# Dense operands at multiples of 512 bytes, per-head sums from two fp32r parts, and new work estimates for the weave

## The chip, the cores and the metric

One core of one Trainium2 chip runs the whole program in one launch. The metric is the device time of one execution in microseconds (us); of several executions the median counts. Smaller is better.

## The reference, cut to what matters

Two transformer blocks in a row, 512 tokens, width 1024, everything in fp32. The first has compressed, selected and windowed attention, a second attention over indexed keys, and a squared-ReLU feed-forward of 4096. The second has a half-weighted SwiGLU feed-forward of 2816, a mixer, and another such SwiGLU. The mixer is what matters for the change, because in it totals over the 64 features of each head are taken again and again:

```python
q = rms_norm_2(sb_q.reshape(B, S, SB_HEADS, HEAD_DIM), sb_q_norm[l])
k = rms_norm_2(sb_k.reshape(B, S, SB_HEADS, HEAD_DIM), sb_k_norm[l])
o_sb = stick_breaking_attention(q, k, v)
o_sb = rms_norm_2(o_sb, sb_out_norm[l].reshape(SB_HEADS, HEAD_DIM)).reshape(B, S, SB_WIDTH)
...
kk = kk / jnp.maximum(jnp.linalg.norm(kk, axis=-1, keepdims=True), 1e-12)
y = rwkv7_recurrence(r, heads(decay), kf, v, -kk, kk * a)
mean = jnp.mean(y, axis=-1, keepdims=True)
var = jnp.mean(jnp.square(y - mean), axis=-1, keepdims=True)
bonus = jnp.sum(r * kf * r_k.astype(jnp.float32), axis=-1, keepdims=True) * v
```

All the rest of the work that matters here is products of 512 tokens with weight matrices.

## The kernel before, in words

**Dense products.** Activations lie transposed, 128 features by 512 tokens to a tile. Each fp32 operand is split in two fp32r parts (high, and low as the remainder), and a product is made of three: high by high, high by low, low by high. `dense` (L352) and `dense_steps` (L362) issue them; a weight block of 128x128 is the stationary operand and an activation tile of 128x512 the moving one. All go through `mm` (L336), so in the profile all have line L339 and are told apart by their tiles: `hh`/`hl` are parts of block inputs, `oh`/`ol` of attention outputs, `uh`/`ul` and `vh`/`vl` of the two kinds of hidden feed-forward tiles, `whi`/`wlo` of weights. `Stream` (L201) loads 1 MB of weights at a time on SP's queue into one of two buffers, ScalarE copies 128x1024 of it to `whi` (L243), VectorE subtracts for `wlo` (L249), one chunk ahead.

The dense work, in blocks of 192 products (8 output tiles, 8 input tiles, 3 products each): 1.875 for the first block's projections from `h` (15 tiles of 24), 1 for its output projection (half of it from tiles of another pool, see below), 8 for the first feed-forward (4 from `hh`/`hl`, 4 from `uh`/`ul`), for each SwiGLU 5.5 up and gate (from `hh`/`hl`) and 2.75 down (from `vh`/`vl`), 3.25 for the mixer's projection and 1 for its output, both from `hh`/`hl`.

**Where tiles lie.** Memory of a partition is given out in stacks, one from the low end and one from the high end ("right"). Every tile is rounded up to 32 bytes. Adding up the tiles gives where each begins, as bytes past a multiple of 512:

- Low end: 16,512 bytes of constants and scratch, then the pool `cst` of 2,368 bytes, so the weight buffers `p32`, the parts `whi`/`wlo` (`phl`), and the temporaries `tmp` begin at 448. Above them in block 1's feed-forward come `x` and `y` at 448, then `g1` (L1280) of 32 bytes, so `uh`/`ul` begin at 480. In the SwiGLU there is no such tile, and `vh`/`vl` begin at 448.
- High end: `hp` with the 16 tiles `hh`/`hl` begins at 480 (it also holds the second half of `oh`/`ol`). Under it lies `cst1` with `gs` (L675), and under that, in block 1 only, `gp` with the first half of `oh`/`ol`, which begin at 0.

**The mixer.** `mix2` (L1681) weaves several chains of small steps with dense products as fillers. The order is made at build time by `weave` (L425): it keeps a modelled clock, to which `mm` adds each product's estimated time and `after` (L468) each step of another engine, runs the chain whose next step is due, and fills with dense products in between, so that these are used up evenly over an estimated amount of chain work, `WORK` (L23), one number for each of five stages. Chains are `rw_solve` (L1809), `rw_scan` (L1962), `sb_steps`' `norm` (L1460), `stick_head` (L1523) and `stick_out` (L1586). Each takes totals over the heads' features as a product with `blk`, a 128x128 matrix of two blocks of ones (tile `c` in the profile, being a slice of the constant table `c2`, L1687): 20 times in `root` (L491), which then forms a reciprocal root with ScalarE and VectorE, 4 times in `rw_solve` for the bonus (L1869), 4 times in `rw_scan` for the mean (L2015). `blk` and what it multiplies are plain fp32, and each such product is two passes. Only one `root` is in progress at a time (`self.roots`), and its temporaries come from 5 buffers used in turn (`tmp`, L605).

The two lines that split and multiply, and the one that takes a total:

```python
self.mm(ps, wh, xh, start=first and k == 0)
self.mm(ps, wh, xl)
self.mm(ps, wl, xh, stop=last and k == n - 1)
...
self.mm(ss, self.blk, x, start=True, stop=True)
```

Of the kernel before, what the change touches and what calls it, by code (L numbers as in the profile page):

```python
# [9 lines left out]
F32 = mybir.dt.float32  # L10
F32R = mybir.dt.float32r
BF = mybir.dt.bfloat16
I32 = mybir.dt.int32
AF = mybir.ActivationFunctionType
OP = mybir.AluOpType
# [3 lines left out]
T = 512  # L19
LA = 1  # L20
TICK, BUSY = 1707, 2100
BURST, MINR = 4, 0.002
WORK = (31e3, 43e3, 45e3, 43e3, 90e3)  # L23
SEM, SEM2, MINF = 250, 50, 4
COST = {"V": (60, 1.07), "S": (60, 0.86), "P": (60, 2.3)}
LHV = (0, 1, 2)
# [267 lines left out]
class K:  # L294
# [196 lines left out]
    def root(self, bank, x, scale, eps, floor=None):  # L491


        V, S = self.nc.vector, self.nc.scalar
        yield lambda: self.roots < 1
        self.roots += 1
        ss = self.bank(bank)
        self.mm(ss, self.blk, x, start=True, stop=True)
        v, l, r = (self.tmp(n) for n in ("rs_v", "rs_l", "rs_r"))
        if floor is None:  # L500
            S.activation(v, ss, AF.Identity, scale=scale, bias=eps)
            w = self.after("S", 512)
        else:
            V.tensor_scalar(v, ss, floor, None, op0=OP.max)
            w = self.after("V", 512)
        S.activation(l, v, AF.Ln)
        S.activation(r, l, AF.Exp, scale=-0.5)
        S.activation(l, r, AF.Square)
        self.after("S", 512, w)
        yield self.after("S", 1024) + 120  # L510
        V.scalar_tensor_tensor(v, v, -0.5, l, op0=OP.mult, op1=OP.mult)
        yield self.after("V", 512)
        V.scalar_tensor_tensor(r, v, 1.5, r, op0=OP.add, op1=OP.mult)
        yield self.after("V", 512)
        return r

    def rsqrt(self, v, l, r, out=None):
        nc = self.nc
# [83 lines left out]
            for ps, w in zip((pa, pb), ws):  # L602
                self.dense(ps, tuple(p[:, 128 * k:128 * k + 128] for p in w), [x], k == 0, k == n - 1)

    def tmp(self, name, tag="t"):  # L605
        return self.tp.tile([128, T], F32, name=name, tag=tag, bufs={"t": 5, "rt": 2}[tag])

    def dump(self, name, src):
        if name in self.dbg:
# [3 lines left out]
    def setup(self, es):  # L613
        tc, nc, a = self.tc, self.nc, self.a
# [8 lines left out]
        c2 = [1024, 1024]  # L623
# [22 lines left out]
        for n, ks in enumerate(OUT2):  # L646
            m = 8 if len(ks) < 3 else 4
# [4 lines left out]
        cp = self.ces.enter_context(tc.tile_pool(name="cst1", bufs=1, side="right"))  # L652
# [13 lines left out]
        C = {k: cst[:, o:e] for k, (o, e) in COFF.items()}  # L666
# [5 lines left out]
        nc.vector.tensor_copy(cz[:, :, 0:1], self.vec("c", 0, 8).unsqueeze(2))  # L672
        self.cz = cz
        self.modc = cp.tile([128, 48], F32, name="modc")
        self.gs = cp.tile([128, 8], F32, name="gs")  # L675
        wap = self.xin.enter_context(tc.tile_pool(name="wap", bufs=1))
        self.wq = self.xin.enter_context(tc.tile_pool(name="wq", bufs=4))
        self.ada0 = deque()
        for n, u in enumerate((0, 1, 4, 5, 2, 3, 6, 7)):
            t = wap.tile([128, 2048], F32, name=f"wa{u}", tag="wa", bufs=WAB)  # L680
# [5 lines left out]
        V, S = nc.vector, nc.scalar  # L686
        ss = self.bank("o")
# [13 lines left out]
        for nm, src, n in (("identb", C["ident"], 128), ("causalb", C["causal"], 128), ("cmaskb", C["cmask"], 256)):  # L701
            t = (c0 if nm == "identb" else cp).tile([128, n], BF, name=nm)
# [30 lines left out]

    def open_h(self):
        self.hes = ExitStack()
        self.hp = self.hes.enter_context(self.tc.tile_pool(name="hp", bufs=8, side="right"))

    def ada_part(self, cg, bank="s"):
# [170 lines left out]
    def block1_attn(self):  # L909
        tc, nc, a, ws = self.tc, self.nc, self.a, self.ws  # L910
        V, S, P = nc.vector, nc.scalar, nc.gpsimd
        x = self.xT
# [5 lines left out]
        ss, sq = self.ss0  # L918
# [81 lines left out]
        for kq in range(4):  # L1000
            hi, lo = ws.get()
            for k2 in range(2):
                k = 2 * kq + k2
# [125 lines left out]
        for i in (1, 2, 3):  # L1129
            w = work[:, WOFF[i] + 128 * i:WOFF[i] + 128 * i + 128]  # L1130
            P.affine_select(out=w, in_=w, pattern=[[-1, 128]], compare_op=OP.is_ge, fill=FILL, base=0,
                            channel_multiplier=1)
        m8 = self.ap.tile([128, 3, 8], F32, name="m8")
        dmask = self.ap.tile([128, 1152], BF, name="dmask")
        top = deque()

# [132 lines left out]
    def block1_ffn(self, oT):  # L1269
        tc, nc, a, ws = self.tc, self.nc, self.a, self.ws  # L1270
        V, S, P = nc.vector, nc.scalar, nc.gpsimd
# [5 lines left out]
        es = ExitStack()  # L1277
        fp = es.enter_context(tc.tile_pool(name="fp", bufs=1))
        y = [fp.tile([128, T], F32, name=f"y{k}") for k in range(8)]
        g1 = fp.tile([128, 8], F32, name="g1")  # L1280
        V.tensor_tensor(g1, self.modc[:, 16:24], self.vec("g_post_mix", 0, 8), op=OP.mult)
        self.gain("g_pre_ffn", 32)

# [16 lines left out]
        t = self.small("ssx")  # L1300
# [14 lines left out]
        for k in range(8):  # L1315
            t, t2 = (fp.tile([128, T], F32, name=n, tag=n, bufs=XB) for n in ("xr", "xg"))
# [364 lines left out]
    def mix2(self):  # L1681
# [2 lines left out]
        es = ExitStack()  # L1684
        cp = es.enter_context(tc.tile_pool(name="cst2", bufs=1))
        self.o2p = self.rpool = cp
        c2 = cp.tile([128, CARR2.shape[1]], F32, name="c2")  # L1687
        nc.scalar.dma_start(c2, a["cst2"])
        C = {k: c2[:, o:e] for k, (o, e) in COFF2.items()}
        self.C2 = C  # L1690
        mb = cp.tile([128, MARR.shape[1]], BF, name="mb")
        for o in range(0, MARR.shape[1], T):
# [2 lines left out]
            nc.scalar.dma_start(m[:, :e - o], a["mask2"][:, o:e])  # L1695
            V.tensor_copy(mb[:, o:e], m[:, :e - o])
        C.update({k: mb[:, o:e] for k, (o, e) in MOFF.items()})
        self.blk = C["blk"]
        self.sbmask = cp.tile([128, 128], BF, name="sbmask")
        V.tensor_copy(self.sbmask, C["sbmask"])  # L1700
        self.sbtri = cp.tile([128, 128], F32R, name="sbtri")
# [107 lines left out]
    def rw_solve(self, f, u, ag):  # L1809
# [4 lines left out]
        t2 = self.rt  # L1814
# [14 lines left out]
        for half in (0, 1):  # L1829
# [9 lines left out]
            S.activation(w(ee), pv[:, :, 1], AF.Exp)  # L1839
            for _ in range(3):  # L1840
                self.after("S", 256)
        dec = t2("dec", 8)
        V.tensor_copy(dec, ch(ei)[:, :, 63])
        yield x

# [17 lines left out]
        r = u[f, 0]  # L1863
        V.scalar_tensor_tensor(bo, r, self.vec("rw_r_k_2", f), kf, op0=OP.mult, op1=OP.mult)
        yield self.after("V", 512)
        yield lambda: (f, 2) in u
        v = u[f, 2]
        ss = self.bank("c")
        self.mm(ss, self.blk, bo, start=True, stop=True)  # L1869
        vt = tok(2, v)  # L1870
        ar = self.rp.tile([128, 8, 2, 64], F32, name="ar", tag="ar", bufs=2)
        V.tensor_tensor(ar[:, :, 1], ch(r), ch(ei), op=OP.mult)
# [89 lines left out]
    def rw_scan(self, f, u, o, g2, sg, w):  # L1962
# [48 lines left out]
                st = ns  # L2011

        yield x
        m = self.bank("pt")
        self.mm(m, self.blk, y, start=True, stop=True)  # L2015
        V.scalar_tensor_tensor(y, m, -1.0 / 64, y, op0=OP.mult, op1=OP.add)
        yield lambda: not self.squares
        self.squares = 1
# [57 lines left out]
```

## Time and profile before

| what | value |
|---|---|
| median of 3 runs | 1977.7 us (1977.63 to 1981.84) |
| the profiled execution's own time | 1968.61 us |
| its span | 1966.8 us |
| PE busy | 1890.1 us, 96% of the span |
| DVE, ACT, POOL busy | 1077.4, 781.3, 149.5 us |
| granted TensorE clock, mean | 0.983 |

The span runs from the first to the last instruction of the program; the time has 1.8 us more around it. PE is TensorE's matmuls, PEld its weight loads, DVE VectorE, ACT ScalarE, POOL GpSimd. The end of a matmul is modelled, so the length of one says little; how far apart the starts of a run of them lie is what counts. In the chain of waits, a stretch of equal products stands as one line with start, length and count, and length over count is the spacing. A line of code belongs to all its instructions, so products are told apart by tiles.

### The profile page before, as it was taken

The numbers are of one execution on the slowest core, as the hardware profiler recorded it, in microseconds if no ns is written. First come the engines' busy times: TensorE is split into PE (matmuls) and PEld (weight loads), VectorE is DVE, ScalarE is ACT, GpSimd is POOL, SyncE is SP. The second block draws the span as 40 slices with busy tenths as digits, with TensorE's granted clock in tenths as the row PEclk, the third lists the DMA queues.
The fourth block names the chain that finished last, engine by engine and source line by source line (L and its number), as shares of the span: only waits on it lengthen the run. The fifth ranks groups of instructions, "written<-read, shape, count | busy, mean of one in ns | idle before, by whom it ended". The sixth has DMA issues, their size and how long they took to land.

```text
span 1966.8 us, 27713 instructions
## 1 busy us (share of the span) xinstructions
PE 1890.1 (96%) x11556; PEld 1446.8 (74%) x11556; DVE 1077.4 (55%) x1814; ACT 781.3 (40%) x1357; POOL 149.5 (8%) x117
## 2 busy tenths in 40 slices
PE   5989999989999998999999999999999999999999
PEld 2766666768888886788888877776666778888887
DVE  7588875573334345543443456666677674344343
ACT  3666777343323133322222354242345652222221
POOL 3341110040000001000000000000002300000000
PEclk8999999989999998999999999999999999999999
DMA  7124124312223222222223231011010023232322
GB/s 298 57 94 134 74 67 148 122 50 91 102 86 107 86 88 83 72 100 87 106 86 107 72 129 61 30 42 45 23 34 33 22 86 107 86 107 86 101 86 91
DMA packets 27342, 171.56 MB, mean 87 GB/s; under 512 B 3152, under 2 KB 3408, under 8 KB 9040
## 3 DMA queue, kind: packets, MB, share of 16 engines
q1 hardware_dynamic: 23472, 163.44, 23.7%
q10 hardware_dynamic: 3744, 6.34, 1.0%
q8 instruction: 91, 1.49, 0.3%
q14 instruction: 35, 0.29, 0.0%
HBM read 167.67 MB, written 2.10 MB: 86 GB/s over the span
## 4 chain that ended last, share of the span: by engine, by line
PE 79%; DVE 3%; ACT 2%; issue 1%; POOL 1%; DMA 0%; POOLq 0%; ACTq 0%; DVEq 0%
PE ps_mm L339 44%; PE ps_s L339 23%; PE ps_c L339 6%; PE ps_pt L339 4%; PE ps_o L339 1%; PE ps_pt L890 1%; POOL xr L1320 0%; DVE wlo L249 0%; ACT whi L243 0%; POOL x L1369 0%; DMA x<-in_x 0%; PE ps_mm L746 0%; DVE hl L1384 0%; DVE y L1368 0%; POOL hl L1327 0%
## 5 line engine op out<-in xcount | busy, mean ns | idle before, releaser
L243 ACT ACTIVATE whi<-w 128x1024 fp32r<-128x1024 f32 (+4 forms) x277 | 274.7, 994 | 771.3 <-PE ps_mm L339 466.1
L339 PE MATMUL ps_mm<-hh,whi 128*128 128x512 f32 x1304 | 526.8, 405 | 21.4 <-ACT whi L243 9.1
L339 PE MATMUL ps_mm<-hh,wlo 128*128 128x512 f32 x1304 | 526.6, 404 | 6.1 <-DVE wlo L249 6.1
L339 PE MATMUL ps_mm<-hl,whi 128*128 128x512 f32 x1304 | 526.6, 404 | 3.2 <-DVE hl L1327 1.5
L249 DVE TENSOR_TENSOR wlo<-w,whi 128x1024 fp32r<-128x1024 f32 (+7 forms) x316 | 321.8, 1026 | 158.3 <-ACT whi L243 157.9
L339 PEld LDWEIGHTS ps_mm<-hh,whi 128*128 128x128 f32 x1304 | 247.0, 190 | 89.2 <-ACT whi L243 12.4
L339 PEld LDWEIGHTS ps_mm<-hh,wlo 128*128 128x128 f32 x1304 | 247.2, 190 | 73.4 <-DVE wlo L249 9.9
L339 PEld LDWEIGHTS ps_mm<-hl,whi 128*128 128x128 f32 x1304 | 247.0, 189 | 69.2 <-issue 4.7
L339 PE MATMUL ps_s<-vl,whi 128*128 128x512 f32 x352 | 137.2, 390 | 0.0
L339 PE MATMUL ps_s<-vh,wlo 128*128 128x512 f32 x352 | 137.0, 389 | 0.0
L339 PE MATMUL ps_s<-vh,whi 128*128 128x512 f32 x352 | 136.8, 389 | 0.0
L1425 DVE TENSOR_TENSOR su<-ps_mm,rr 128x512 f32<-128x512 f32 x42 | 29.0, 690 | 139.8 <-PE ps_mm L339 139.8
L1437 DVE SCALAR_TENSOR_TENSOR x<-ps_s,x 128x512 f32<-128x512 f32 x48 | 33.2, 691 | 129.2 <-PE ps_s L339 129.2
L339 PE MATMUL ps_s<-uh,wlo 128*128 128x512 f32 x256 | 101.1, 395 | 0.0
L339 PE MATMUL ps_s<-uh,whi 128*128 128x512 f32 x256 | 101.1, 395 | 0.0
L339 PE MATMUL ps_s<-ul,whi 128*128 128x512 f32 x256 | 101.1, 395 | 0.0
L1424 DVE TENSOR_TENSOR sg<-ps_mm,rr 128x512 f32<-128x512 f32 x42 | 29.0, 691 | 103.9 <-PE ps_mm L339 99.7
L339 PEld LDWEIGHTS ps_s<-vl,whi 128*128 128x128 f32 x352 | 66.1, 188 | 14.3 <-DVE vl L771 0.6
L339 PEld LDWEIGHTS ps_s<-vh,wlo 128*128 128x128 f32 x352 | 66.1, 188 | 13.9
L339 PEld LDWEIGHTS ps_s<-vh,whi 128*128 128x128 f32 x352 | 66.1, 188 | 13.8
L1361 DVE TENSOR_TENSOR y<-y,ps_s 128x512 f32<-128x512 f32 x24 | 16.5, 687 | 74.0 <-PE ps_s L339 74.0
L339 PEld LDWEIGHTS ps_s<-uh,wlo 128*128 128x128 f32 x256 | 48.0, 187 | 11.8
(569 smaller groups left out, 2710.2 us busy)
## 6 DMA issues: line engine op xcount, KB each, us to landing
w<-in_gu SPq DMA_DIRECT2D x44, 1024.0 KB, 4.9
w<-in_win SPq DMA_DIRECT2D x17, 1024.0 KB, 5.0
w<-in_wada SPq DMA_DIRECT2D x16, 1024.0 KB, 5.4
w<-in_wup SPq DMA_DIRECT2D x16, 1024.0 KB, 4.9
w<-in_wdn SPq DMA_DIRECT2D x16, 1024.0 KB, 4.9
w<-in_dn SPq DMA_DIRECT2D x16, 1024.0 KB, 4.9
wa<-in_wada SPq DMA_DIRECT2D x8, 1024.0 KB, 13.6
w<-in_dn SPq DMA_DIRECT2D x8, 768.0 KB, 4.3
```

The costliest lines, as they stand in the source:

```text
L243: self.nc.scalar.activation(hi[:, :n], src, AF.Copy)
L249: self.nc.vector.tensor_tensor(lo[:, o:m], src[:, o:m], hi[:, o:m], op=OP.subtract)
L339: self.last_pe = self.nc.tensor.matmul(o, l, r, start=start, stop=stop, skip_group_check=True)
L890: nc.tensor.transpose(b[:, x:x + 128], p[:, po:po + 128], self.ident)
L1361: V.tensor_tensor(y[m], y[m], ps, op=OP.add)
L1424: V.tensor_tensor(g, pg, r, op=OP.mult)
L1425: V.tensor_tensor(v, pu, r, op=OP.mult)
L1437: V.scalar_tensor_tensor(self.x[m], ps, 0.5, self.x[m], op0=OP.mult, op1=OP.add)
```

## The change

- **Layout.** `gs` grows from 32 to 64 bytes, `m8` from 96 to 128, `g1` from 32 to 512; a pool of 480 bytes is put above `hp`; `dec` (twice 32 bytes) moves from the mixer's pool into `cst`. The constant table `c2` is cut in two: its first 1,536 bytes go into a temporary and only the rest stays, while `blk` gets 512 bytes of its own. By the same sums `whi`/`wlo`, `hh`/`hl`, `oh`/`ol`, `uh`/`ul` and `vh`/`vl` now all begin at 0 past a multiple of 512.
- **Totals.** `head_sums` splits the tile in a high and a low fp32r part (a ScalarE copy, a VectorE subtraction, two temporaries) and multiplies `blk`, now fp32r, with each. It takes the place of the fp32 product in all 28 places. In `rw_solve` it comes before the wait for the value tile instead of after it.
- **Estimates.** The five numbers of `WORK` go down by 3,000 to 5,000.

```diff
-WORK = (31e3, 43e3, 45e3, 43e3, 90e3)
+WORK = (28e3, 40e3, 41e3, 40e3, 85e3)
...
-        ss = self.bank(bank)
-        self.mm(ss, self.blk, x, start=True, stop=True)
+        ss = yield from self.head_sums(bank, x)
...
+    def head_sums(self, bank, x):
+        hi, lo = (self.tmp(n, dt=F32R) for n in ("hs_h", "hs_l"))
+        self.nc.scalar.activation(hi, x, AF.Copy)
+        yield self.after("S", 512)
+        self.nc.vector.tensor_tensor(lo, x, hi, op=OP.subtract)
+        yield self.after("V", 512)
+        ss = self.bank(bank)
+        self.mm(ss, self.blk, hi, start=True)
+        self.mm(ss, self.blk, lo, stop=True)
+        return ss
...
-        self.gs = cp.tile([128, 8], F32, name="gs")
+        self.gs = cp.tile([128, 16], F32, name="gs")[:, :8]
...
+        self.hes.enter_context(self.tc.tile_pool(name="pad", bufs=1, side="right")).tile([128, 120], F32, name="pad")
...
-        m8 = self.ap.tile([128, 3, 8], F32, name="m8")
+        m8 = self.ap.tile([128, 4, 8], F32, name="m8")[:, :3]
...
-        g1 = fp.tile([128, 8], F32, name="g1")
+        g1 = fp.tile([128, 128], F32, name="g1")[:, :8]
...
-        c2 = cp.tile([128, CARR2.shape[1]], F32, name="c2")
-        nc.scalar.dma_start(c2, a["cst2"])
-        C = {k: c2[:, o:e] for k, (o, e) in COFF2.items()}
+        n1 = COFF2["cum"][0]
+        c1 = self.tmp("c1")
+        nc.scalar.dma_start(c1[:, :n1], a["cst2"][:, :n1])
+        c2 = cp.tile([128, CARR2.shape[1] - n1], F32, name="c2")
+        nc.scalar.dma_start(c2, a["cst2"][:, n1:])
+        C = {k: c1[:, o:e] if o < n1 else c2[:, o - n1:e - n1] for k, (o, e) in COFF2.items()}
...
-        self.blk = C["blk"]
+        self.blk = cp.tile([128, 128], F32R, name="blk")
+        V.tensor_copy(self.blk, C["blk"])
...
-        dec = t2("dec", 8)
+        dec = self.small("dec", 8)
...
+        ss = yield from self.head_sums("c", bo)
         yield lambda: (f, 2) in u
         v = u[f, 2]
-        ss = self.bank("c")
-        self.mm(ss, self.blk, bo, start=True, stop=True)
...
-        m = self.bank("pt")
-        self.mm(m, self.blk, y, start=True, stop=True)
+        m = yield from self.head_sums("pt", y)
```

## Rows read from the trace of the kernel before

**Rows 1.** The page: span, busy time of each engine.

```profile
span 1966.8 us, 27713 instructions
PE 1890.1 (96%) x11556; PEld 1446.8 (74%) x11556; DVE 1077.4 (55%) x1814; ACT 781.3 (40%) x1357; POOL 149.5 (8%) x117
```

**Rows 2.** Stretches: start:end, length, busy of PE, PEld, DVE, ACT, POOL, clock, DMA.

```profile
0.00:341.00 341.00, 300.34 (x1694) 208.88 (x1694) 245.91 (x560) 218.40 (x488) 80.70 (x67) 0.96 0.35 126
...
419.00:767.00 348.00, 347.96 (x1484) 279.44 (x1484) 138.54 (x153) 105.73 (x136) 6.72 (x4) 0.99 0.27 94
...
808.00:1152.00 344.00, 344.00 (x1490) 278.98 (x1489) 154.34 (x184) 99.96 (x120) 0.00 (x0) 1.00 0.27 95
...
1191.00:1450.00 259.00, 257.10 (x3899) 184.57 (x3898) 172.99 (x358) 93.85 (x191) 0.00 (x0) 1.00 0.11 37
1450.00:1570.00 120.00, 115.08 (x755) 81.84 (x754) 83.78 (x169) 71.78 (x148) 29.23 (x24) 0.99 0.09 30
...
1607.00:1963.00 356.00, 355.94 (x1544) 288.47 (x1542) 150.22 (x177) 94.50 (x111) 0.00 (x0) 1.00 0.27 94
```

**Rows 3.** The chain that ended last: start, length, engine, tile, line, count.

```profile
453.72 44.80 PE ps_s L339 x192
498.52 44.80 PE ps_mm L339 x192
...
875.55 43.55 PE ps_s L339 x192
919.10 89.60 PE ps_mm L339 x384
```

**Rows 4.** Timeline of PE, first block's output projection: start, length, instruction.

```profile
349.64 0.39 PE L339 MATMUL ps_mm<-oh,whi 128*128 128x512 f32 x1
...
352.39 0.40 PE L339 MATMUL ps_mm<-oh,whi 128*128 128x512 f32 x1
...
355.18 0.39 PE L339 MATMUL ps_mm<-oh,whi 128*128 128x512 f32 x1
```

**Rows 5.** The same view in the mixer: one total, and what follows it.

```profile
1200.40 1.02 PE L339 MATMUL ps_c<-bo,c 128*128 128x512 f32 x2
1201.35 1.15 PE L339 MATMUL ps_c<-ident,u 64*64 64x64 f32 x32
```

**Rows 6.** Groups by line and tile: totals' passes, a root's step, a split.

```profile
L339 PE MATMUL ps_c<-bo,c x8: 592/592/697, 1200.4 to 1397.8; 128*128 128x512 f32 x8
...
L506 ACT ACTIVATE rs_l<-rs_v 128x512 f32<-128x512 f32 x20 | 12.6, 628 | 2.6 <-DVE rs_v L504 2.2
...
L1617 ACT ACTIVATE hh<-orw x4: 620/622/631, 1467.1 to 1495.7; 128x512 fp32r<-128x512 f32 x4
...
L1619 DVE TENSOR_TENSOR hl<-orw,hh x4: 677/684/1220, 1468.9 to 1496.3; 128x512 fp32r<-128x512 f32 x4
L1619 DVE TENSOR_TENSOR hl<-sq,hh x4: 681/954/1523, 1525.0 to 1577.7; 128x512 fp32r<-128x512 f32 x4
```

**Rows 7.** The chain that ended last, in the mixer's last stage.

```profile
1541.72 0.83 DVE rs_v L511
...
1543.15 0.60 DVE rs_r L513
```

**Rows 8.** Weight loads, the constants' load and copy, and ACT's longest wait.

```profile
w<-in_gu SPq DMA_DIRECT2D x44, 1024.0 KB, 4.9
...
c<-in_cst ACTq DMA_DIRECT2D x1, 320.0 KB, 2.8
...
L1702 DVE CAST sbtri<-c x1: 219/219/219, 1155.4 to 1155.4; 128x128 fp32r<-128x128 f32 x1
...
ACT whi L243 <- PE ps_mm L339: 466.1, 147, 9.5
```

More of the change, by code (lines that the diff above doesn't have):

```diff
@@ L603, in dense2, with tmp @@
                 self.dense(ps, tuple(p[:, 128 * k:128 * k + 128] for p in w), [x], k == 0, k == n - 1)
-    def tmp(self, name, tag="t"):
-        return self.tp.tile([128, T], F32, name=name, tag=tag, bufs={"t": 5, "rt": 2}[tag])
+    def tmp(self, name, tag="t", dt=F32):
+        return self.tp.tile([128, T], dt, name=name, tag=tag, bufs={"t": 5, "rt": 2}[tag])
     def dump(self, name, src):
```

## The prediction

> **What bounds the kernel now.** I read the page first. TensorE (PE) is busy for 96% of the span, VectorE for 55%, ScalarE for 40% [rows 1]: a change counts as far as it shortens what PE does, or makes PE wait. Then the stretches [rows 2]. In the first feed-forward and both SwiGLUs PE has no idle time (344.00 of 344.00 us in the third row), while VectorE is busy for under half; in the mixer from 1191 to 1450 PE is busy for 257.10 of 259.00. Two stretches differ: the first 341 us (PE 300.34) and the mixer's end, 1450 to 1570 (PE 115.08 of 120, with VectorE at 83.78). The granted clock is 1.00 in the full ones, the upper level, 2.4 GHz. The supply isn't late: a megabyte of weights lands in 4.9 us and feeds 48 products, some 11 us of PE, and ScalarE waits 466.1 us in all for PE before it may split more weights [rows 8].
>
> So the spacing of dense products matters, and the chain of waits gives it in blocks of 192 [rows 3]. The reader is to see two prices for the same work. The blocks from `uh`/`ul` and from `hh`/`hl` take 44.80 us, 233.3 ns a product. The block from `vh`/`vl` at 875.55 takes 43.55 us, 226.8 ns. Line, shapes and types are the same, both `ps_s` blocks have the same loop around them, and the weights begin at 448 in all; what differs is that `uh`, `ul`, `hh`, `hl` begin at 480 past a multiple of 512 bytes and `vh`, `vl` at 448. The output projection shows a third place [rows 4]: its first 12 products come from tiles at 0, and (352.39 - 349.64) / 12 = 229.2 ns; the next 12, from tiles at 480, take (355.18 - 352.39) / 12 = 232.5 ns. The floor is a column a cycle, 512 / 2.4 = 213.3 ns, 40.96 us a block; no row comes near it.
>
> **Layout: the first and largest term.** After the change both operands begin at 0. No row shows that pair. Moving at 480 with weights at 448 is 233.3, 448 with 448 is 226.8, 0 with 448 is 229.2. Bounds: 213.3 ns below (no loss at all), 233.3 above (the place doesn't matter). I take 226.8. The pair (0, 0) is nearest to (448, 448) in the one thing that orders the three rows: there moving and stationary operand begin at the same place in a 512-byte stretch, and that row is the fastest; moving one alone to 0 made it worse, so 0 by itself has no merit that a row shows. Then:
> - `hh`/`hl`/`uh`/`ul` blocks in full stretches: 8 in the first feed-forward, 2 x 5.5 in the SwiGLUs, 3.25 and 1 in the mixer, 23.25; each saves 44.80 - 43.55 = 1.25 us.
> - First block's projections, 1.875 blocks, and half of its output projection: PE isn't always the bound there, so half of 2.375 counts, 1.2.
> - `vh`/`vl`, 5.5 blocks: already at 226.8, nothing.
>
> 24.45 x 1.25 = **30.6 us saved**. With faster products the splits must keep up; VectorE and ScalarE have half of each full stretch free, so nothing is late next.
>
> **Totals from two parts.** Removed: 28 fp32 products of two passes. The two records of one span 1.02 us and one lasts 592 ns [rows 5, 6], so the passes are 0.43 apart, 0.86 in all; from its start to the next product's it is 0.95, hand-over included. I take 0.86. Added: two fp32r products, 2 x 0.227 = 0.45. PE saves 0.41 each. Added beside PE: a ScalarE copy, 0.62 as at L1617, and a VectorE subtraction, 0.68 as at L1619 in the median, both in front of the sum, so each chain step grows by 1.30 less 0.41. In a full PE stretch the fillers cover that: 20 of the 28 lie in 1191 to 1450, where the additions raise VectorE from 173 to 187 us of 259. There 20 x 0.41 = 8.1 us are saved. The other 8 lie in 1450 to 1570, where the chain runs through VectorE steps of roots in places [rows 7]; PE's 3.3 us are saved at most, 8 x 1.30 = 10.4 are added at most. I take half of the 10.4 as exposed, 2 us net lost. Sum: **6.1 saved**; bounds 11.4 saved (all hidden) and 2.3 lost (the end fully exposed). The five `root` temporaries now fill the ring of 5 buffers once; a write could wait for the reader five tenants back. Such a wait would sit on ScalarE or VectorE ahead of the weight splits, and it lies inside the bound above as long as PE has split weights in hand.
>
> **Estimates.** The modelled clock changes the order alone. PE's idle time in the two weave stretches is 1.9 and 4.9 us; better pacing can remove at most these 6.8, worse pacing may add about as much again. I take nothing.
>
> **Constants.** One load becomes two on ScalarE's queue, and `blk` is copied once more by VectorE: 0.22 us as `sbtri` [rows 8], beside PE. If the new load landed late, VectorE's queue would hold the splits behind the copies for up to another 2.8 us. I take nothing: in the trace that load lands 2.8 us after its issue [rows 8], with PE running meanwhile. `dec`, `m8`, `gs`, `g1` and the pad change addresses only.
>
> **Sum.** 30.6 + 6.1 = 36.7 us. Against the profiled execution's own time: 1968.6 - 36.7 = 1931.9. The median of the runs stands 9.1 above that execution; the same saving from the median gives **1941 us**. A measurement here tells about 0.2% (4 us) from no change.
>
> **Rivals.**
> - *No loss at 0 (faster than forecast).* If what costs 13 to 20 ns over 213.3 is that an operand begins away from 0, both being there takes it away. For it: every weight tile in the trace is off 0, so no row contradicts it. Against: moving one operand to 0 cost 2.4 ns more than 448. At the floor 24.45 x 3.84 + 5.5 x 2.59 = 108, with totals 114: 1864 us; half way to the floor 69 and 6: 1902. Chance 0.32. The Trainium skill, TensorE: Matmul & The Clock Gate, Back-to-back issue gap, gives N / 2.4 + 2.5 ns for a warm product, 215.7 for 512 columns; the trace disagrees (226.8 at best), and by that page's figure the time would be an estimated 1877.
> - *The place gives little.* If 0 acts as in [rows 4], 229.2 ns, the 24.45 blocks save 0.80 each and the 5.5 lose 0.45: 17 and 6, 1955 us. If it gives nothing, only the totals are left: 1972. For it: the one row with an operand at 0. Against: that row has weights at 448. Chance 0.12. The Trainium skill, SBUF — State Buffer, Specifications (TRN2), has lines of 16 bytes; by that, 480, 448 and 0 are equally good, and the time would be 1972. The trace disagrees: 44.80 against 43.55.
> - *The longer totals become the bound of the weave (slower).* Copy and subtraction stand in front of all 28 sums, one root at a time. For it: a like subtraction took up to 1523 ns in the mixer's end [rows 6]. Exposed at that length a total costs 0.62 + 1.52 - 0.41 = 1.73 us, all 28 of them 48.4: 1977.7 - 30.6 + 48.4 = 1996. It decides from 18 exposed totals on. Against: 20 of 28 lie where PE always has fillers. Chance 0.06.
>
> **How the numbers follow.** Forecast 0.50 (its own range 1928 to 1955: the totals' and pacing bounds, with the runs' own spread), no loss 0.32, little 0.12, slower 0.06. The range for 8 in 10 reaches from near the floor, 1866, to 1956, the better half of "little". Faster by over 0.2%: the first two and most of the third, 0.91. Within 0.2%: 0.03. Slower: 0.06.
>
> **What would show it.** Right: blocks of 192 at 43.5 us in the chain for all tile names, the first feed-forward's stretch near 338 us instead of 348, 56 fp32r products with `blk` in place of 56 fp32 passes, PE still without idle time from 1191 to 1450. Blocks at 41 to 42 mean the first rival, 44.0 or more the second. PE idle time in the mixer that grows past some 15 us, behind ScalarE copies or VectorE subtractions of the totals, means the third. The forecast is wrong if blocks at (0, 0) are not near 43.55.

## The result, and the profile after

The changed kernel takes **1955.6 us** in the median of 4 runs (1951.5 to 1957.0) against 1979.8 for the kernel before (4 runs): ratio 0.987, 95% interval [0.985, 0.990], 24 us less. A second set on another occasion gave 1960.0 against 1976.7, ratio 0.991 [0.990, 0.993]. The forecast was 36.7 us less, 1941; both results are faster than before by more than a measurement tells, and by less than forecast. The first lies outside the forecast's own range (1928 to 1955) and 0.4 us inside the range for 8 in 10 (up to 1956), the second outside both.

The page of the changed kernel, its span and busy times, against [rows 1]:

```profile
span 1949.7 us, 27795 instructions
PE 1864.8 (96%) x11552; PEld 1456.1 (75%) x11556; DVE 1094.1 (56%) x1843; ACT 797.5 (41%) x1385; POOL 149.9 (8%) x117
```

TensorE lost 25 us of busy time, but the span only 17.1: 8 us of new idle time. Which stage it is shows in the chain that ended last (start, length, engine, tile, line, count), against [rows 3]:

```profile
450.44 43.52 PE ps_s L339 x192
493.96 43.52 PE ps_mm L339 x192
...
861.98 43.52 PE ps_s L339 x192
905.50 87.04 PE ps_mm L339 x384
```

Every block of 192 dense products now takes 43.52 us, 226.7 ns a product, whatever tile it reads; the forecast took 226.8. So the loss is not in the dense stages. The time itself, 1955.6, is that of the rival "the place gives little" (1955), but these blocks rule that rival out: it needs 44.0 us or more. The stretches show it (start:end, length, busy time and instructions of PE, PEld, DVE, ACT, POOL, granted clock, DMA share, GB/s), against [rows 2]:

```profile
417.01:755.00 337.99, 337.99 (x1484) 279.58 (x1484) 138.59 (x153) 105.81 (x137) 6.70 (x4) 1.00 0.29 97
796.70:1133.97 337.27, 337.27 (x1489) 279.03 (x1488) 154.31 (x183) 99.74 (x120) 0.00 (x0) 1.00 0.28 97
1133.97:1608.44 474.47, 457.14 (x5010) 336.64 (x5010) 325.88 (x651) 229.47 (x453) 29.57 (x24) 0.98 0.14 46
1171.00:1431.00 260.00, 251.03 (x3738) 185.62 (x3736) 179.70 (x368) 106.91 (x213) 0.00 (x0) 0.99 0.11 37
1431.00:1551.00 120.00, 114.32 (x884) 84.48 (x885) 87.97 (x173) 70.85 (x147) 29.57 (x24) 0.94 0.06 21
```

The first feed-forward's stretch is 338.0 us where 348 stood, the SwiGLU 337.3 where 344 stood, both with TensorE busy throughout. The third row is the whole mixer, from the end of the first SwiGLU's last block to the first block of the second. It takes 474.5 us, against 466.7 (1152.3 to 1619.0) in the profiled execution of before; the forecast's terms (5.3 from the layout, 6.1 from the totals) make it 455.3. Inside it, the weave's stretch now has 260.00 - 251.03 = 9.0 us of idle TensorE (1.9 before), and in the mixer's end the granted clock is 0.94 (0.99 before).

So the span's 17.1 us are 2.0 before the first feed-forward, 9.6 up to the SwiGLU, 6.7 and 6.5 in the two SwiGLUs, 24.8 in all, less 7.8 lost in the mixer. The runs below ask where those 7.8, and the 11.4 that were forecast there, went.

To compare mixers, each is split in three: TensorE's idle time; what the clock cost (the mixer cut into stretches of 5 us, each one's length times one minus its granted clock, summed); and the rest, the work at the upper level, 2.4 GHz (with whatever short waits the modelled ends of matmuls hide). In us, one profiled execution a row:

| kernel | mixer | idle | clock | rest |
|---|---|---|---|---|
| before | 466.7 | 8.4 | 1.7 | 456.6 |
| before, profiled again | 473.9 | 8.2 | 10.3 | 455.5 |
| layout alone | 470.7 | 8.8 | 6.8 | 455.0 |
| layout and estimates | 469.8 | 10.8 | 3.4 | 455.6 |
| totals alone | 473.2 | 14.6 | 8.5 | 450.1 |
| changed, old estimates | 474.2 | 16.7 | 8.6 | 448.9 |
| **changed** | 474.5 | 17.4 | 10.3 | 446.9 |
| changed, profiled again | 479.9 | 17.2 | 17.2 | 445.6 |
| low parts on GpSimd | 483.1 | 21.7 | 13.7 | 447.7 |
| `bo` totals undone | 464.7 | 12.9 | 3.4 | 448.5 |
| `bo` and `y` totals undone | 465.3 | 12.7 | 3.4 | 449.2 |

### The profile page after: what moved, and what is told of

It reads as the page before. It is cut to its first block, busy times and chain, and to the rows that moved or that the text cites. A ratio compares the mean times of both kernels' runs of the same rounds, so it can differ in the third digit from the quotient of the medians.

```text
span 1949.7 us, 27795 instructions
## 1 busy us (share of the span) xinstructions
PE 1864.8 (96%) x11552; PEld 1456.1 (75%) x11556; DVE 1094.1 (56%) x1843; ACT 797.5 (41%) x1385; POOL 149.9 (8%) x117
## 4 chain that ended last, share of the span: by engine, by line
PE 77%; DVE 3%; ACT 2%; POOL 1%; issue 1%; DMA 1%; ACTq 0%; POOLq 0%
PE ps_mm L339 43%; PE ps_s L339 23%; PE ps_c L339 5%; PE ps_pt L339 4%; PE ps_o L339 1%; ACT whi L243 1%; DVE wlo L249 1%; POOL xr L1332 0%; PE ps_pt L902 0%; POOL x L1381 0%; DMA mask<-in_mask 0%; DMA x<-in_x 0%; PE ps_mm L758 0%; DVE hl L1396 0%; DVE rs_v L510 0%
## 5 line engine op out<-in xcount | busy, mean ns | idle before, releaser
L339 PE MATMUL ps_mm<-hh,whi 128*128 128x512 f32 x1304 | 519.9, 400 | 20.9 <-ACT whi L243 9.5
L339 PE MATMUL ps_mm<-hh,wlo 128*128 128x512 f32 x1304 | 518.1, 398 | 6.2 <-DVE wlo L249 6.2
L339 PE MATMUL ps_mm<-hl,whi 128*128 128x512 f32 x1304 | 519.2, 398 | 3.4 <-DVE hl L1339 2.0
L339 PEld LDWEIGHTS ps_s<-vh,wlo 128*128 128x128 f32 x352 | 66.1, 188 | 13.7
L339 PEld LDWEIGHTS ps_s<-vh,whi 128*128 128x128 f32 x352 | 66.1, 188 | 13.7
L876 ACT ACTIVATE P<-ps_s,st 128x512 f32<-128x512 f32 (+2 forms) x96 | 50.1, 528 | 15.7 <-DVE st L874 13.8
```

The source lines that it names most:

```text
L339: self.last_pe = self.nc.tensor.matmul(o, l, r, start=start, stop=stop, skip_group_check=True)
L876: nc.scalar.activation(p[:, po:po + n], b[:, o:o + n], AF.Exp, bias=st[:, i:i + 1], accum_out=st[:, 4 + i:5 + i])
```

## Experiments

### One part at a time

Layout alone, with the totals and estimates of before (`root` shown; the totals of `bo` and `y` likewise):

```diff
-WORK = (28e3, 40e3, 41e3, 40e3, 85e3)
+WORK = (31e3, 43e3, 45e3, 43e3, 90e3)
...
-        ss = yield from self.head_sums(bank, x)
+        ss = self.bank(bank)
+        self.mm(ss, self.blk, x, start=True, stop=True)
...
-        self.blk = cp.tile([128, 128], F32R, name="blk")
+        self.blk = cp.tile([128, 128], F32, name="blk")
```

> The changed layout alone: totals again as one fp32 product, the work estimates again those of before. In the changed kernel the dense stages shortened as forecast (blocks of 192 at 43.52 us) but the mixer grew from 466.7 to 474.5 us, where 11.4 less was forecast. Theory A, the two-part totals cost PE waits in the weave: here the mixer falls to some 461 us and the whole to about 1948 us (before 1979.8 less 31). Theory B, the new estimates place the fillers worse: the same 1948. Theory C, the mixer's chain on VectorE and ScalarE sets its length, whatever PE does: mixer 467 or more, whole about 1955, near the changed kernel.

Measured: 1952.9 us against 1975.8 (17 runs of before, shared by these four), ratio 0.988 [0.987, 0.990], 22.9 less. Its mixer:

```profile
1135.14:1605.82 470.68, 461.85 (x5010) 333.00 (x5010) 309.15 (x623) 213.74 (x426) 29.14 (x24) 0.99 0.14 47
```

Layout and new estimates, the diff above without its first two lines:

> Changed layout and new estimates, totals again as one fp32 product. Theory A (totals): as the layout alone, about 1948 us, mixer near 461. Theory B (estimates): the loss is here, about 1958 us, mixer near 472. Theory C (chain): near 1955 like the layout alone.

Measured: 1949.3, ratio 0.987 [0.985, 0.988].

The changed kernel with the old estimates alone:

> The changed kernel with the estimates of before. Theory A (totals): no gain, 1953 to 1960 us, mixer still over 470. Theory B (estimates): about 1942 us, mixer near 455. Theory C (chain): 1955, nothing moves.

Measured: 1952.4, ratio 0.988 [0.986, 0.989].

The totals alone, without the layout:

```diff
-        self.gs = cp.tile([128, 16], F32, name="gs")[:, :8]
+        self.gs = cp.tile([128, 8], F32, name="gs")
...
-        self.hes.enter_context(self.tc.tile_pool(name="pad", bufs=1, side="right")).tile([128, 120], F32, name="pad")
...
-        m8 = self.ap.tile([128, 4, 8], F32, name="m8")[:, :3]
+        m8 = self.ap.tile([128, 3, 8], F32, name="m8")
...
-        g1 = fp.tile([128, 128], F32, name="g1")[:, :8]
+        g1 = fp.tile([128, 8], F32, name="g1")
```

(`WORK` as before, too; `dec` stays where the change puts it, so the split weights begin at 0, with `hh`, `hl` at 480 and `uh`, `ul` at 32, 32 bytes either side: the blocks take 44.80 us as in [rows 3].)

> Two-part totals alone, on the old places of the tiles and with the old estimates. Theory A (totals): slower than before by 8 to 16 us, 1988 to 1996, all of it in the mixer, with PE idle time there above 15 us. Theory B (estimates): faster than before by 6 us, 1974, as forecast for the totals. Theory C (chain): the same as before or up to 5 us slower.

Measured: 1975.5 (12 runs), ratio 0.999 [0.998, 1.000].

```profile
1153.61:1626.78 473.17, 458.64 (x5009) 335.32 (x5008) 322.36 (x651) 228.10 (x454) 28.89 (x24) 0.98 0.14 47
```

What follows. **The layout carries the whole gain**: 22.9 us alone, about the 24.8 of the dense stages. **The totals give nothing**: they take 6 us of work off the mixer (rest 450.1 for 456) and put 6 us of idle time in (14.6 for 8.4) on the old layout; on the new one it is 6.1 off and 7.9 in. The estimates' effect lies within the intervals. Theory A's sign is nearly there, 14.6 us of idle time or more with the totals and under 11 without, but alone they cost no 8 to 16 us, and even the layout alone leaves the mixer at 470.7 where A had 461. Theory C's numbers fit both runs; its reason, a chain that sets the length whatever TensorE does, does not, since with the layout alone TensorE is idle for only 8.8 us of the mixer. The last part of this section gives another.

### Is the profiled execution of before a typical one?

The kernel before, unchanged:

> The kernel before, unchanged, profiled once more. Its first profile is at a mean granted clock of 0.983 and 1968.6 us, under all of its 17 timed runs (1969.4 to 1981.5). If that execution met fewer dips of the clock than usual, this one has a mean clock near 0.978, a mixer of 470 to 474 us instead of 466.7 with the same PE idle time of some 8.4 us, and the dense blocks at 44.80 and 43.55 us again. If the difference lies elsewhere, the mixer is 466 to 468 again.

Measured: 1980.2 us, mean clock 0.977, blocks at 44.80 and 43.55, and

```profile
1156.69:1630.61 473.92, 465.79 (x5009) 334.06 (x5009) 308.95 (x622) 213.88 (x426) 29.25 (x24) 0.98 0.14 47
1501.69:1531.69 30.00, 28.38 (x106) 18.63 (x105) 19.12 (x38) 16.15 (x32) 9.26 (x8) 0.72 0.08 27
```

Its idle time (8.2 for 8.4) and its rest (455.5 for 456.6) are nearly those of the first profile; the clock costs 8.6 us more, 10.3 in all, and 8.4 of these lie in the 30 us of the second row, granted 0.72 on the mean between the two levels. The first execution met almost none of that: at 1968.6 us it lies under all 17 runs of the first set. So two profiles of one kernel differ by 7 us in the mixer, through the clock.

The changed kernel, unchanged:

> The changed kernel itself, unchanged, beside the kernel before on this chip: 1951 to 1957 us, ratio about 0.987; its mixer with 16 to 18 us of PE idle time and several dips of the clock again, 472 to 476 us, if those belong to its order of work and not to one execution.

Measured: 1960.0 (5 runs) against 1976.7, ratio 0.991 [0.990, 0.993]. The profile:

```profile
1137.51:1617.38 479.87, 462.73 (x5009) 341.32 (x5009) 325.21 (x651) 230.14 (x453) 29.49 (x24) 0.96 0.14 46
```

The same 17 us of idle time, and the clock takes 17.2, longer than expected. Taken set by set, first with first and second with second, the changed mixer is 6 to 8 us longer than that of before; across the sets it is 1 to 13.

### Where the totals' idle time comes from

In the changed kernel's waits of TensorE in the mixer (us in total, times, longest) the first three are

```profile
PE ps_c L339 <- DVE z L1955: 3.2, 4, 1.9
PE ps_c L339 <- DVE hs_l L521: 2.9, 1, 2.9
PE ps_c L339 <- DVE tmt L1968: 2.3, 4, 1.2
```

where the kernel before has, of these three,

```profile
PE ps_c L339 <- DVE z L1940: 0.4, 1, 0.4
```

The middle one is a total's low part, in a single wait, and the timeline shows it (start, length, engine, line, instruction; in brackets the idle time before it):

```profile
1183.88 0.74 DVE L1880 SCALAR_TENSOR_TENSOR bo<-u,vecs,u 128x512 f32<-128x512 f32 x1
...
1184.65 0.63 ACT L519 ACTIVATE hs_h<-bo 128x512 fp32r<-128x512 f32 x1 [1.52 <-DVE bo L1880]
...
1185.74 0.40 PE L339 MATMUL ps_c<-hs_h,blk 128*128 128x512 f32 x1
1185.74 0.69 DVE L1895 SCALAR_TENSOR_TENSOR ar<-kk,ee 128x512 f32<-128x512 f32 x1
...
1185.98 0.41 PE L339 MATMUL ps_c<-hs_l,blk 128*128 128x512 f32 x1
...
1186.22 0.40 PE L339 MATMUL ps_c<-hs_h,blk 128*128 128x512 f32 x1
1186.35 0.68 DVE L1466 TENSOR_TENSOR sq<-ps_mm,rr 128x512 f32<-128x512 f32 x1
...
1188.75 0.69 DVE L521 TENSOR_TENSOR hs_l<-bo,hs_h 128x512 fp32r<-128x512 f32 x1
...
1189.49 0.51 PE L339 MATMUL ps_c<-hs_l,blk 128*128 128x512 f32 x1 [2.87 <-DVE hs_l L521]
```

The products at 1185.74 and 1185.98 are a total as it was forecast: 0.24 us each, 0.48 for the pair (0.45 forecast, 0.86 before). The next one, of `bo`, has its high part ready at 1185.28, but its subtraction begins at 1188.75: five other instructions of VectorE, `ar`, `sq`, a half of `wlo`, `kk` and another half, stand in front of it. The order of TensorE's products is fixed when the kernel is built, so it holds 2.87 us between two products that belong together.

But this is 2.9 of the 9 us of new idle time, and no other total shows such a wait. The other two stand behind `z` and `tmt`, steps of `rw_solve` that take no total. The largest of them come where the weave has put no fillers:

```profile
1428.11 0.50 PE L339 MATMUL ps_mm<-hh,wlo 128*128 128x512 f32 x1
...
1431.76 0.69 PE L339 MATMUL ps_c<-tmt,am 64*64 64x64 f32 x32 [1.22 <-DVE tmt L1968]
...
1437.74 1.15 PE L339 MATMUL ps_c<-tmt,z 64*64 64x64 f32 x32 [1.85 <-DVE z L1955]
...
1438.82 0.50 PE L339 MATMUL ps_mm<-hh,whi 128*128 128x512 f32 x1
```

Between the first and the last of these rows no dense product stands, and TensorE idles for 3.4 us; in the kernel before, two to four of them stand between every two steps of the same solve (1438 to 1447). With the old estimates the waits behind `z` are there too, 3.9 us in seven pieces. So the totals also cost through the order of work that they change; which of their steps does it was not tried. Two runs ask whether the one wait is the queue's.

The low parts moved to GpSimd:

```diff
-        self.nc.vector.tensor_tensor(lo, x, hi, op=OP.subtract)
-        yield self.after("V", 512)
+        self.nc.gpsimd.tensor_tensor(lo, x, hi, op=OP.subtract)
+        yield self.after("P", 512)
```

> The changed kernel with the low part of each total (x - hi) made by GpSimd in place of VectorE. In the changed kernel TensorE waited 2.87 us for one low part that stood behind five VectorE instructions, and was idle for 17.4 us of the mixer against 8.4 before. Theory A (the low parts stand in VectorE's queue, and push its other work back): idle time falls to 9 to 12 us, mixer to some 466 us, the whole to about 1948. Theory C (it is the longer chain of each total, two more instructions, that counts): a GpSimd subtraction is longer than 0.68 us, so the idle time stays at 17 us or grows, the whole 1955 or more.

Measured: 1961.5 (6 runs), ratio 0.993 [0.991, 0.994], 21.7 us idle. The groups of the low part:

```profile
L521 POOL TENSOR_TENSOR hs_l<-hsq,hs_h 128x512 fp32r<-128x512 f32 x12 | 16.0, 1331 | 517.7 <-ACT hs_h L519 517.7
L521 POOL TENSOR_TENSOR hs_l<-qx,hs_h 128x512 fp32r<-128x512 f32 x8 | 13.4, 1679 | 84.7 <-ACT hs_h L519 75.1 <-DVE rs_v L510 9.6
```

Off VectorE's queue the subtraction takes 1.3 to 1.7 us instead of 0.68, and the idle time grows, as theory C had it. At the `bo` total itself the queue is gone, and the wait falls from 2.87 to 1.29 us:

```profile
1185.98 1.77 DVE L1880 SCALAR_TENSOR_TENSOR bo<-u,vecs,u 128x512 f32<-128x512 f32 x1
...
1188.62 1.58 POOL L521 TENSOR_TENSOR hs_l<-bo,hs_h 128x512 fp32r<-128x512 f32 x1 [1.42 <-PE ps_c L339]
...
1190.26 0.49 PE L339 MATMUL ps_c<-hs_l,blk 128*128 128x512 f32 x1 [1.29 <-POOL hs_l L521]
```

So the queue made more than half of that one wait. For the rest the run can't part queue from chain, for it lengthens the subtraction as it moves it, and a VectorE instruction that ran beside one took longer too (`bo` 1.77 us here, 0.74 above).

The `bo` totals as one fp32 product, the other 24 in two parts:

```diff
+        self.blk1 = cp.tile([128, 128], F32, name="blk1")
+        V.tensor_copy(self.blk1, C["blk"])
...
-        ss = yield from self.head_sums("c", bo)
         yield lambda: (f, 2) in u
         v = u[f, 2]
+        ss = self.bank("c")
+        self.mm(ss, self.blk1, bo, start=True, stop=True)
```

> The changed kernel with the four totals of bo (one a period of the weave) as one fp32 product again, the other 24 still from two parts. Theory A' (only the bo total is badly placed, the wait of 2.87 us): TensorE idle in the mixer falls from 17.4 to about 13 us, products cost 4 x 0.41 = 1.6 more, the whole about 1952. Theory A (all totals crowd VectorE): idle stays at 15 or more, no change.

Measured: 1946.3 us, ratio 0.985 [0.983, 0.987], idle 12.9.

```profile
1135.77:1600.51 464.74, 451.88 (x5010) 332.08 (x5010) 323.88 (x648) 226.11 (x450) 29.50 (x24) 0.99 0.14 47
```

Undoing 4 of 28 totals takes 4.5 us of idle time away, as theory A' said, and costs 1.6 to 2.9 of work; and the clock's part falls from 10.3 and 17.2 to 3.4, which no theory had said.

The four means of `y` undone too (the same two lines in place of `head_sums("pt", y)`), so that the 20 roots alone have two parts:

> The changed kernel with the totals of bo and the four means of y as one fp32 product, only the 20 roots from two parts. In the run with the four totals of bo alone put back, the mixer fell to 464.7 us and the whole to 1946.3. Theory A (low parts in VectorE's queue make TensorE wait wherever the chain has no cover): 1 to 3 us better again, 1944. Theory A' (only the bo total was badly placed): 1947 or 1948, four times 0.41 us more of products and nothing gained.

Measured, beside the changed kernel on the same chip: **1942.5 us** (1941.9 to 1946.5) against 1960.0 and, for the kernel before, 1976.7; ratio 0.983 [0.982, 0.985].

```profile
1133.92:1599.19 465.27, 452.60 (x5010) 332.21 (x5010) 318.87 (x644) 223.13 (x446) 29.78 (x24) 0.99 0.14 47
```

This version beats both kernels. Its time is the one that theory A named (1944), but its idle time (12.7 for 12.9) and clock are those of the run before it, so the gain that A meant is not seen, and the four `y` decide nothing that these runs can tell (the two intervals overlap). What the roots are worth shows against layout and estimates without any two-part total: 6.4 us less work, 1.9 more idle, 4.5 net in the mixer, one profile against one.

Why the clock falls more in the changed kernel's profiles than with `bo` undone is not settled. The stretch ahead of the dip that both profiles of the changed kernel have, 185 us into the mixer:

```profile
1313.97:1318.97 5.00, 3.81 (x48) 2.49 (x46) 3.55 (x8) 3.26 (x7) 0.00 (x0) 1.00 0.00 0
1318.97:1323.97 5.00, 4.02 (x66) 2.95 (x66) 3.18 (x10) 1.42 (x5) 0.00 (x0) 0.71 0.01 3
1323.97:1328.97 5.00, 5.00 (x66) 3.77 (x66) 2.81 (x7) 0.82 (x2) 0.00 (x0) 0.60 0.01 3
```

and the same place with `bo` undone:

```profile
1315.77:1320.77 5.00, 3.68 (x52) 2.57 (x48) 3.70 (x8) 2.87 (x8) 0.00 (x0) 1.00 0.00 0
1320.77:1325.77 5.00, 4.92 (x65) 3.39 (x66) 4.18 (x9) 0.85 (x3) 0.00 (x0) 1.00 0.01 3
```

In the changed kernel TensorE idles for 2.2 us of these 10, and its second stretch holds no dense filler at all; with `bo` undone it idles for 1.4 and the second stretch holds seven, and the clock stays at the upper level. Over the table's rows the clock costs 8.5 to 17.2 us in the five profiles with `bo` in two parts and 1.7 to 10.3 in the six others. The two groups overlap, and those five are also the five with the most idle time.

The mean granted clock is on record for the timed executions too, and there the tendency does not hold. It is 0.978 for the kernel before (37 executions) and with the layout alone (5), but 0.980 with the totals alone (12), which have `bo` in two parts; it is 0.978 and 0.976 in the changed kernel's two sets, 0.980 with `bo` undone and 0.982 with `y` undone too. So on the old layout `bo` in two parts does not lower the clock, and what does in the changed kernel stays open. Over the 37 executions of before, 0.001 of clock goes with 1.9 us of time (a line through them). By that, as an estimate, 12 of the 17 us between the changed kernel and the last version on one chip are the clock's, and so are all 4 us between the changed kernel's own two sets.

### What about a place makes a product fast

Places are bytes past a multiple of 512. First, weights at 448, and each of the moving buffers 32 bytes further than its neighbour:

```diff
-        return (self.hp.tile([128, T], F32R, name="hh", tag="hh"), self.hp.tile([128, T], F32R, name="hl", tag="hl"))
+        return tuple(self.hp.tile([128, T + 8], F32R, name=n, tag=n)[:, :T] for n in ("hh", "hl"))
...
-                uh = fp.tile([128, T], F32R, name="uh", tag="uh", bufs=10)
-                ul = fp.tile([128, T], F32R, name="ul", tag="ul", bufs=10)
+                uh, ul = (fp.tile([128, T + 4], F32R, name=n, tag=n, bufs=10)[:, :T] for n in ("uh", "ul"))
...
-        dec = self.small("dec", 8)
+        dec = t2("dec", 8)
```

(and without `pad`, and with `g1` of 8 columns)

> The changed kernel with its split weights back at 448 past a multiple of 512 bytes, and each of the buffers of hh, hl, uh, ul 32 bytes further than the one before it, so that the moving operands of the feed-forwards begin at all sixteen multiples of 32. Read: the spacing of products in the feed-forward stretches by the place of the moving operand. Theory S (the two operands must begin at the same place): 226.7 ns for a moving tile at 448 alone, 229 to 233 ns elsewhere. Theory M (the moving operand must begin at a multiple of 64 bytes): 226.7 ns at 0, 64, ... 448, and 233.3 ns at 32, 96, ... 480, whatever the weights' place. Theory Z (a multiple of 512): no place is as fast as 226.7 but 448 or 0.

Measured: 1976.9 us in one run, the layout's gain gone. Its chain, a block from `uh`/`ul`, one from `hh`/`hl`, one from `vh`/`vl`, which stayed at 448:

```profile
453.04 44.51 PE ps_s L339 x192
497.55 44.65 PE ps_mm L339 x192
...
873.76 43.56 PE ps_s L339 x192
```

Mixed places cost 232 ns on the mean. Spacings by place (from a product's start to the next one's, in the records of the first feed-forward): 0 233.4, 64 233.0, 128 230.5 ns in `hh`, and 448 225.0 in `hl`, but 320 225.7 there as well. So theory M falls: multiples of 64 are not the fast ones. S is not clean either, for a product's neighbours differ from it in place here, and a spacing belongs to two products: counted from the start before, the one at 448 is the slowest of all, 240.7.

Then with the split weights spread as well (buffers of 1032 columns in place of 1024):

> As the run with weights at 448, but the split weights' buffers too are 32 bytes apart from each other, at 0, 32, 64 and 96 past a multiple of 512 in the feed-forwards. Theory S: the fast cells are those where moving tile and weights have the same place (0 with 0, 64 with 64), 226.7 ns, all others 229 to 233. Theory M: 226.7 ns in every cell whose moving tile is at a multiple of 64, 233.3 in the others; weights at 32 or 96 cost nothing. Theory W (the weights' place counts as the moving one's does): weights at 32 and 96 add some 6 ns to the products that load them.

Every block takes 44.5 to 44.7 us, the whole 1983.1, and the places' medians lie between 228 and 238 ns without order. Theories M, W and, as far as a mixed sequence can tell, S get no support: with everything mixed, everything costs 232.

So the last kernel keeps each tag at one place: weights at 480, `hh`/`hl` at 480, `uh`/`ul` at 448, `vh`/`vl` at 32:

```diff
+        c0.tile([128, 8], F32, name="cpad")
...
-        self.hes.enter_context(self.tc.tile_pool(name="pad", bufs=1, side="right")).tile([128, 120], F32, name="pad")
...
-        g1 = fp.tile([128, 128], F32, name="g1")[:, :8]
+        g1 = fp.tile([128, 120], F32, name="g1")[:, :8]
...
         fp = es.enter_context(tc.tile_pool(name="fp2", bufs=1))
+        fp.tile([128, 16], F32, name="vpad")
...
-        dec = self.small("dec", 8)
+        dec = t2("dec", 8)
```

> The changed kernel with other places: split weights at 480 past a multiple of 512 bytes, hh and hl at 480 too, uh and ul at 448 (32 before the weights), vh and vl at 32 (64 past the weights). Theory S (moving operand and weights at the same place are the fast case, the place itself is free): blocks from hh and hl 43.52 us, blocks from uh, ul and vh, vl slower, 44 to 45. Theory Z (a multiple of 512, or of 64, is needed): blocks from hh and hl 44.8 us as before, those from uh at 448 the faster ones.

Measured: 1962.6 us in one run. The chain:

```profile
452.00 44.80 PE ps_s L339 x192
496.80 43.55 PE ps_mm L339 x192
...
868.74 43.96 PE ps_s L339 x192
912.71 87.09 PE ps_mm L339 x384
```

`ps_mm` is from `hh`/`hl`: 43.55, fast at 480 with 480. The first `ps_s` is from `uh`/`ul` at 448, 44.80; the second from `vh`/`vl` at 32, 43.96. **Theory S holds where each tag has one place**: what counts is the distance from the weights' place to the moving operand's. At distance 0 it is 226.7 to 226.9 ns, in all of 0, 448 and 480; 32 either way 233.3; +64 gives 43.96 / 192 = 229.0, as [rows 4] had with 0 and 448. Why mixed places cost 232 whatever the distance stays open, and whether 512 is the period was not tried.

### Why the layout gave nothing in the mixer

The mixer's fillers come in short runs between other products. One of four, with the layout alone:

```profile
1241.85 0.50 PE L339 MATMUL ps_mm<-hh,whi 128*128 128x512 f32 x1
1242.19 0.40 PE L339 MATMUL ps_mm<-hl,whi 128*128 128x512 f32 x1
1242.43 0.40 PE L339 MATMUL ps_mm<-hh,wlo 128*128 128x512 f32 x1
1242.66 0.40 PE L339 MATMUL ps_mm<-hh,whi 128*128 128x512 f32 x1
1242.99 0.33 PE L339 MATMUL ps_pt<-uc,tok 64*64 64x64 f32 x4
```

1242.66 - 1242.19 = 0.47 for two, 235 ns each. Over the run's 564 spacings between mixer fillers (those under 260 ns, so without the first of a run, which takes about 0.34 us), the median after the second product of a run is 232 ns, after the third 234, then 232, 231, and from the sixth on 227. In the kernel before it was 229, 231, 235, 233, then 234. A run of four gains nothing; only long runs reach 227, and 265 of the 564 come that late in a run. On the mean of all, the spacing went from 232.5 to 230.3 ns, about 1.2 us over these products.

## Why the forecast was right or wrong

- **Layout, 30.6 us.** The price was exact: 226.7 for 226.8 ns, and for the reason given, that both operands begin at the same place; the run at 480 with 480 shows it. The first feed-forward gave 9.6 us (10 forecast), the SwiGLUs 13.2 (13.75), the first stage 2.0 (1.5, being 1.2 blocks). The mixer's 4.25 blocks, 5.3 us, failed: the price was read from blocks of 192 in a row, while most fillers there stand in runs too short for it. The mixer's rest fell by 1.6 us at most (455.0 and 455.6 for 455.5 and 456.6).
- **Totals, 6.1 us.** The step that failed is "in a full PE stretch the fillers cover that". The saving at TensorE was right in kind: 6 us of work less, where 28 x 0.41 = 11.5 were counted; where the other 5.5 went no run shows, for a pair by itself costs 0.48 as forecast. But idle time grew by as much as the work fell, and the totals alone changed the time by -0.3 us (interval -4 to +1). The stretch's 1.9 us of idle time held for the old order of work; in the new one it has 9.0, so the sign "PE still without idle time from 1191 to 1450" failed. Of the whole mixer's 17.4 (8.4 before), 2.9 stand behind one low part and 5.5 behind two other steps of the solves, some of it where no fillers stand. I counted the added instructions' durations, 1.30 us, and neither what stands in front of them (a subtraction of 0.68 us came 3.5 us after its operand) nor that the weave would deal the fillers out anew; "worse pacing may add about as much again" stood in the prediction as a bound, and I took nothing. The two `yield`s in front of the `bo` total also hold back all that `rw_solve` issues after it, which I did not count; that this, more than the queue, is what the undone `bo` gave back was not tried apart.
- **Clock.** No step of the forecast had it. In the profiled mixers it cost 10.3 and 17.2 us in the changed kernel, 1.7 and 10.3 in the one before, 3.4 with `bo` undone. The forecast rested on a profile with nearly none, and by adding the difference of 9.1 to the median it carried that over as if it were fixed.
- **Estimates and constants, nothing.** With and without the new estimates the times agree within their intervals. The constants were not tried by themselves.
- **Rivals.** "No loss at 0" is out: 43.52, not 41. (The Trainium skill, TensorE: Matmul & The Clock Gate, Back-to-back issue gap, by whose formula for one warm product such a block would be an estimated 41.4 us: no block of any run came nearer than 43.52.) "The place gives little" is out in the dense stages. (The Trainium skill, SBUF — State Buffer, Specifications (TRN2), with lines of 16 bytes, would have all these places equal; 32 bytes made 43.55 into 44.80.) "The longer totals become the bound of the weave" had its sign half met: TensorE's idle time passed the 15 us named, 17.4 in all, but only 2.9 of it stands behind a total's low part, and it is 9 us more than before, not 48.

In the sum of the two first profiles: 24.8 us from dense stages; in the mixer 9.7 less work (456.6 to 446.9) against 9.0 more idle time and 8.6 more of clock. Of the medians, the second set's 16.7 us less is after some 4 us lost to the clock (0.976 against 0.978, by the estimate above).

## What to carry to other kernels

Put both operands of back-to-back products at the same distance past a multiple of 512 bytes; read the price from the chain's blocks, and use it for long runs alone. A cheaper product that needs two more steps on other engines paid here at the roots and not at `bo`; before counting its price, look at what stands in front of the added step in its queue, at what its own stream issues behind it, and at where a woven order then puts its fillers. And before the sum is made against one profile, see where its clock dipped: one more profile of the same kernel shows how much of a stage is luck.

## What the runs showed of the hardware that was not expected

- With each operand at one place throughout, the spacing of dense fp32r products went by the distance between the two places and not by the places: 226.7 to 226.9 ns at 0 (three pairs), 229.0 and 229.2 at +64 (two), 233.3 at 32 either way; 232 when places are mixed.
- In the mixer, the fast spacing takes some five products of a run to set in: 231 to 234 ns up to the fifth, 227 from the sixth.
- One kernel's mixer lost 1.7 us to the clock in one execution and 10.3 in another, at nearly the same idle time (8.4 and 8.2); over 37 executions of that kernel the mean granted clock lay between 0.976 and 0.982 and the time between 1981.6 and 1969.4.
- GpSimd needs 1.3 to 1.7 us for a 128x512 subtraction that VectorE does in 0.68, and a VectorE instruction beside it took 1.77 us instead of 0.74.
